# A one-core transformer block with routed experts: ranks from two tiles' counts, normed rows kept on the chip, final half rows loaded last, new order numbers

## The chip, the cores and the metric

The kernel runs on one core of a Trainium2 chip. The metric is device time in microseconds, from the first instruction to the last with what the launch adds; the median of three runs is compared. The core has five engines with queues of their own: PE (TensorE, matrix products), DVE (VectorE), ACT (ScalarE), POOL (GpSimd) and SP (SyncE, which here issues nearly all loads and stores). A queue runs strictly in its order: what stands behind a waiting instruction waits too. 16 DMA engines carry the transfers.

## What is computed

One layer on 1024 latent tokens of 1024 numbers, with 256 context tokens. A normed and modulated input goes through one projection, three groups of token mixers (windowed attention, gated mixing in chunks, differential attention) and an output projection with a gated residual. Behind that stand routed experts and a final norm; the change lies in this half:

```python
y = jnp.concatenate([ya, yb, yc], axis=-1) @ w_out
x = x + gt1 * y
h2 = rmsnorm(x, g_ffn[l]) * (1.0 + sc2) + sh2
...
pg = jax.nn.softmax((t @ w_rg) + b_rg, axis=-1)       # 4 groups, the best one
ptop, gsel = lax.top_k(pg, 1)
...
lv, li = lax.top_k(le_g, MOE_TOPK)                    # 2 of its 4 experts
for e in range(N_EXPERTS):                            # 16
    he = jax.nn.silu(t @ w_gate[e]) * (t @ w_up[e])   # 1024 -> 512
    y = y + gates[:, e:e + 1] * (he @ w_down[e])      # 512 -> 1024
...
x = x + gt2 * y
return rmsnorm(x, g_final)
```

All is float32; products are made exact enough by splitting an operand into a high and a low part, three products for one.

## The kernel before

The first half (to 586.9 us) is the same in both versions. The second half is recorded as steps by `add(engine, estimated us, (key, class), function, reads, writes)`. `Plan.order` then replays them as a list scheduler: of the steps that are ready it takes the one with the least start time plus `weight * (key + shift[class])`, the shifts being the table `SHIFT2`, and writes the instructions of all engines in that order. `key` is a due time by place in the program. Buffers are rings: `F` (1024 columns, 6), `R` (raw weight slabs, 7), `W` (split slabs, 31), `XP`, `he`, `C`, and in PSUM `A` and `T`.

*Tiles.* `out_tile(t)`, eight times 128 tokens: transposes (`turn`, L1081), the output projection as two halves of eight steps of `three` products (L1075 to L1077, two halves n), gate and residual (L1158, L1160), squares on ACT (L1166), inverse root on POOL (L1171 to L1173), norm and modulation on DVE (L1176, L1179), a store of the residual to `accd` (L1169) and of the normed rows to `h2d` (L1180). Then the router: transposes of the normed rows, logits (L1197), group and expert choice on DVE (L1204 to L1231), running counts per expert in `selsum` (`base`, L1234), places by a product with a triangle (L1238, L1239), slot numbers (L1251 to L1257), and two indirect stores that enter token and gate into `table` (`enter`, L1260). For tiles in `AGAIN = (0, 3, 4)` the router's transposes don't read the normed rows where VectorE wrote them, but a copy loaded back from `h2d`; the buffer is free earlier so.

*Ranks.* Experts are worked on by rank, and each rank has a fixed capacity in token rows, `CAPS`: 320, five times 192, seven times 128, three times 64; a loop behind everything (L1690) takes what does not fit. `first_expert` finds rank 0 from the counts of the first `FIRST = 2` tiles, into `oi0`. `rank_experts` ranks all 16 from the counts of `CUT = 6` tiles, with rank 0 kept, into `oi`. `close` pads rank 0's count to `EARLY = 192` rows, so that two early blocks of rank 0 (128 and 64 rows) can be gathered from the tables of six tiles alone; tile 6's `base` waits for it.

*Experts.* Ranks are taken in the order `ORDER` (0, 9, 13, 8, ...). A rank has 24 slabs of 256 KB (8 gate, 8 up, 8 down), all 384 in one chain on SP (`slab`, L1042). Each is split into high and low, on ACT (L1062) and on DVE or POOL (L1039). `expert_block` handles 128 or 64 rows: SP loads its indices from `table` (L1439, after the tables of all tiles but for the early blocks), POOL gathers the rows from `h2d` (L1442), PE transposes them (L1457), ACT and DVE split them (L1469, L1473), then gate, up (L1075 and so on; L1483, L1486 for 64 rows), SiLU (L1498), the gate factor (L1501), down, and POOL adds the result into `accd` (L1445).

*Tail.* `final_tile(t)` loads `accd` after all sums but those of the last rank, norms it and stores it: tiles 0 to 3 through ring `F`, tile 4 through `C`, tiles 5 to 7 as half rows through `R`. The last rank's block does its rows by itself and scatters them over the output when all stores of the tiles have landed.

## Time and profile before

| | us |
|---|---|
| median of 3 runs | 1183.41 (1179.22 to 1183.45) |
| the profiled execution | 1187.16 |
| its span, first to last instruction | 1185.4 |
| second half, from 586.9 to the end | 598.5 |

The profile is one execution. Busy times say how long an engine executed; an idle time stands in brackets in a timeline's row with what ended it. Positions are microseconds from the span's start, lines are those of the kernel before. The TensorE clock has two levels, 1.2 and 2.4 GHz; PEclk is the granted share of the higher. In the second half a row of SP (`SPq`) is the issue of a transfer, not the transfer.

### The profile page before, as it was taken

To read this page: it belongs to the slowest core of one execution; us is meant where nothing else is said; L and a number is where in the kernel's file an instruction comes from. 1 tells how busy PE (TensorE), PEld (TensorE's weight loads), DVE (VectorE), ACT (ScalarE), POOL (GpSimd) and SP (SyncE) were. 2 spreads that over 40 slices of the span, in tenths; PEclk is the share of its full clock that TensorE was granted. 3 is DMA by queue.
4 is the path that set the end of the run, shared out by engine and by line. 5 is a ranking of instruction groups with operands and counts; after the bars stand their busy time and mean duration, and the time that the engine had idled before them with its cause. 6 is when DMAs were issued, how large, how long until landed. Compare 5 with 4: busy or idle time off the path is not lost. (4 is left out here: it accounts for less than half of the span.)

```text
span 1185.4 us, 18587 instructions
## 1 busy us (share of the span) xinstructions
PE 1055.2 (89%) x5621; PEld 833.7 (70%) x5621; DVE 909.9 (77%) x1735; ACT 718.4 (61%) x1443; POOL 414.3 (35%) x452
## 2 busy tenths in 40 slices
PE   6999999977999999999799985899989989899680
PEld 1688677766888888888677874686767767677550
DVE  6665779748788887887757778889886878988865
ACT  6774122118988888988622332377676667777753
POOL 0200000103778788776522534312222313222220
PEclk9899999999999999999989897899989999999895
DMA  9624674010000000000244663589988988899995
GB/s 326 217 80 148 197 236 152 9 41 9 19 1 19 1 1 19 10 4 7 62 143 159 207 198 133 167 270 294 272 297 265 294 282 263 268 288 292 271 317 219
DMA packets 99980, 191.30 MB, mean 161 GB/s; under 512 B 17720, under 2 KB 19560, under 8 KB 99750
## 3 DMA queue, kind: packets, MB, share of 16 engines
q1 hardware_dynamic: 93574, 172.59, 43.8%
q0 software_dynamic: 6272, 17.51, 6.8%
q8 instruction: 45, 0.74, 0.3%
q14 instruction: 57, 0.47, 0.1%
q10 hardware_dynamic: 32, 0.01, 0.0%
HBM read 168.95 MB, written 24.07 MB: 163 GB/s over the span
## 5 line engine op out<-in xcount | busy, mean ns | idle before, releaser
L698 DVE TENSOR_REDUCE st<-SC 128x1 f32<-128x1280 f32 x64 | 95.2, 1487 | 20.8 <-PE SC L693 16.3
L430 PE MATMUL acc<-wh,hH 128*128 128x512 f32 x256 | 101.2, 396 | 1.7 <-ACT bu L530 0.9
L431 PE MATMUL acc<-wl,hH 128*128 128x512 f32 x256 | 100.8, 396 | 0.0
L432 PE MATMUL acc<-wh,hL 128*128 128x512 f32 x256 | 100.3, 392 | 0.0
L1075 PE MATMUL A<-W,XP 128*128 128x512 f32 x236 | 98.6, 418 | 0.6 <-ACT W L1062 0.6
L1076 PE MATMUL A<-W,XP 128*128 128x512 f32 x236 | 95.6, 405 | 1.8 <-DVE W L1039 1.8
L701 ACT ACTIVATE P<-SC,st 128x1280 f32<-128x1280 f32 x64 | 85.2, 1330 | 16.6 <-DVE st L698 15.4
L1077 PE MATMUL A<-W,XP 128*128 128x512 f32 x236 | 95.0, 403 | 0.0
L1062 ACT ACTIVATE W<-R 128x512 fp32r<-128x512 f32 x111 | 69.0, 626 | 27.4 <-DMA R<-in_w_down_dram 7.0
L1039 DVE TENSOR_TENSOR W<-R,W 128x512 fp32r<-128x512 f32 x102 | 69.8, 694 | 18.3 <-ACT W L1062 16.2
L633 ACT ACTIVATE PT<-T 128x512 f32<-128x512 f32 (+1 forms) x126 | 65.2, 546 | 11.3 <-PE T L629 9.5
L745 PE MATMUL T<-vc,PT 128*128 128x64 f32 x512 | 62.2, 275 | 0.3 <-DVE qa L930 0.2
L1445 POOL DMA_INDIRECT accd<-F,IX x18 | 30.8, 1709 | 87.8 <-DVE F L1504 26.5
L745 PEld LDWEIGHTS T<-vc,PT 128*128 128x128 f32 x512 | 59.7, 192 | 0.6 <-ACT PT L633 0.4
L693 PE MATMUL SC<-KC,QC 128*128 128x512 f32 (+1 forms) x192 | 52.4, 381 | 6.6 <-ACT P L701 6.3
L430 PEld LDWEIGHTS acc<-wh,hH 128*128 128x128 f32 x256 | 48.1, 188 | 13.8 <-issue 2.3
L432 PEld LDWEIGHTS acc<-wh,hL 128*128 128x128 f32 x256 | 48.1, 188 | 11.3 <-issue 1.1
L1075 PEld LDWEIGHTS A<-W,XP 128*128 128x128 f32 x236 | 46.3, 196 | 12.9 <-ACT W L1062 1.3
L431 PEld LDWEIGHTS acc<-wl,hH 128*128 128x128 f32 x256 | 48.1, 188 | 10.3 <-issue 0.9
L857 DVE TENSOR_REDUCE ast<-SA 128x1 f32<-128x640 f32 (+1 forms) x64 | 50.2, 784 | 6.0 <-PE SA L850 5.4
L455 DVE SCALAR_TENSOR_TENSOR macc<-mw,cs,macc 128x512 f32<-128x512 f32 x56 | 41.8, 747 | 16.6 <-DMA mw<-in_w_ada_dram 16.2
L1076 PEld LDWEIGHTS A<-W,XP 128*128 128x128 f32 x236 | 46.2, 196 | 11.7 <-DVE W L1039 2.8
(782 smaller groups left out, 3155.5 us busy)
## 6 DMA issues: line engine op xcount, KB each, us to landing
R<-in_w_gate_dram SPq DMA_DIRECT2D x74, 256.0 KB
R<-in_w_down_dram SPq DMA_DIRECT2D x73, 256.0 KB
R<-in_w_up_dram SPq DMA_DIRECT2D x72, 256.0 KB
mw<-in_w_ada_dram SPq DMA_DIRECT2D x64, 256.0 KB
wr<-in_w_in_dram SPq DMA_DIRECT2D x32, 256.0 KB
kc<-in_w_up_dram SPq DMA_DIRECT2D x20, 256.0 KB
kc<-in_w_down_dram SPq DMA_DIRECT2D x19, 256.0 KB
late_vcB<-in_w_gate_dram SPq DMA_DIRECT2D x18, 256.0 KB
```

Of the source, the lines that this page charges most:

```text
L430: nc.tensor.matmul(acc[:, n0:n1], lhsT=a, rhs=W[k][0][:, n0:n1], start=(k == 0), stop=False)
L431: nc.tensor.matmul(acc[:, n0:n1], lhsT=a, rhs=W[k][1][:, n0:n1], start=False, stop=False)
L432: nc.tensor.matmul(acc[:, n0:n1], lhsT=b, rhs=W[k][0][:, n0:n1], start=False, stop=(k == KD - 1))
L633: nc.scalar.activation(dst, src, AF.Copy)
L698: nc.vector.tensor_reduce(small[0][:, j:j + 1], buf(("SC", u, j))[:, 0:1280], axis=AX.X, op=OP.max, negate=True)
L701: nc.scalar.activation(buf(("P%d" % j, u)), buf(("SC", u, j))[:, 0:1280], AF.Exp, bias=small[0][:, j:j + 1], accum_out=small[0][:, 2 + j:3 ...
L745: nc.tensor.matmul(buf(O)[:, 0:64], lhsT=buf(("PT", u, g))[:, (c - c0) * 128:(c - c0 + 1) * 128], rhs=vc[c // 8][:, c % 8, h * 64:(h + 1) ...
L1039: (nc.gpsimd if engine == "POOL" else nc.vector).tensor_sub(dst, a, b)
L1062: h = add("ACT", 0.525, (key, "sh"), lambda: nc.scalar.activation(buf(value)[:, 0:512], raw(), AF.Copy), r=r, w=[value], after=[chain["spl ...
L1075: nc.tensor.matmul(acc, lhsT=ah, rhs=w[:, 0:512], start=first, stop=False)
L1076: nc.tensor.matmul(acc, lhsT=ah, rhs=w[:, 512:1024], start=False, stop=False)
L1077: nc.tensor.matmul(acc, lhsT=al, rhs=w[:, 0:512], start=False, stop=last)
```

## The change

- `AGAIN` is empty: the router's transposes of all tiles read the rows where VectorE wrote them; three loads go.
- `rank_experts` ranks all 16 experts from the counts of the first two tiles (`NB0`); `first_expert`, `oi0` and `lead` go. `close` takes rank 0's count of six tiles from `NB_`.
- The half rows of the final norm (ring `R`) are recorded as coming after the last slab (`after=[chain["load"]]`).
- Classes get finer: the steps of tile 5 (`c`), tile 7 (`z`), of the early blocks (`a`) and the last rank (`z`) have shifts of their own, as have constants and final tiles. All numbers of `SHIFT2` are new, the weight is 8.4e-05 instead of 0.005541, and some estimated times are set anew.

```diff
-SHIFT2 = dict(weight=0.005541, c=-100.3, fa=-315.5, fh=20.8, fl=78.4, fn=-1857.9, fo=545.6, fr=-845.7, fs=276.2,
...
+SHIFT2 = dict(weight=8.4e-05, c0=7509.6, c1=-814.8, c2=10962, c3=3158.7, c4=-4675.7, ex=3038.8, fa=-107164,
...
-AGAIN, LAGR = (0, 3, 4), 8.8
+AGAIN, LAGR = (), 8.8
...
+            own = {CUT - 1: "c", NT - 1: "z"}.get(t, "")
...
-            add("DVE", 1.2, (k, "oh"), lambda: nc.vector.scalar_tensor_tensor(
+            add("DVE", 1.2, (k, "oh" + own), lambda: nc.vector.scalar_tensor_tensor(
...
-        def first_expert():
...
-            nc.vector.tensor_copy(cnt, buf(NB_)[:, :16])
+            nc.vector.tensor_copy(cnt, buf(NB0)[:, :16])
...
-            nc.vector.scalar_tensor_tensor(key, lead, 65536.0, key, op0=OP.mult, op1=OP.add)
...
-            nc.vector.tensor_scalar(gap, cnt, -1.0, float(EARLY), op0=OP.mult, op1=OP.add)
+            nc.vector.tensor_scalar(gap, buf(NB_)[:, :16], -1.0, float(EARLY), op0=OP.mult, op1=OP.add)
...
-        add("DVE", 1.2, (kc_, "k0"), first_expert, r=[NB0], w=["oi0"])
+        add("DVE", 3.1, (kc_, "k0"), rank_experts, r=[NB0], w=["oi"])
...
-        add("DVE", 5.4, (kc_, "k"), rank_experts, r=[NB_, "oi0"], w=["oi"])
-        add("DVE", 0.4, (kc_, "k"), close, r=["oi"], w=["adj"])
+        add("DVE", 0.6, (kc_, "k"), close, r=[NB_, "oi"], w=["adj"])
...
-                load(n * 1.36e-3, (k, "fl"), lambda Y=Y: buf(Y), lambda c=c: accd[rows, c], [Y], r=["sum"])
+                load(n * 1.36e-3, (k, "gl"), lambda Y=Y: buf(Y), lambda c=c: accd[rows, c], [Y], r=["sum"],
+                     after=[chain["load"]] if ring == "R" else [])
```

VectorE, before, about where tile 6 waits for its places: the end of the ranking (L1316 to L1321), gathered rows of the first early block (`XP`, L1473), closing (L1325 to L1327), tile 6's base (L1234, L1235).

```order
L1316 TENSOR_REDUCE rank<-q_5675 128x16
L1317 TENSOR_TENSOR q_5675<-rank,ie 128x256
L1319 TENSOR_TENSOR q_5676<-q_5675,ie 128x256
L1320 TENSOR_REDUCE order<-q_5676 128x16
L1321 CAST oi<-order 128x16
L1473 TENSOR_TENSOR XP_5631<-T_5658,XP_5631 128x512
L1325 TENSOR_SCALAR gap<-cnt 128x16
L1326 SCALAR_TENSOR_TENSOR gap<-gap,q_5675 128x16
L1327 TENSOR_TENSOR selsum<-selsum,gap 1x16
L1234 CAST sel<-selsum 128x16
```

The same place now (new line numbers): the count of six tiles (L1304), the slots of tile 4 (L1264 to L1270, the numbers behind the names tell the tiles apart), closing, the next tile's slots.

```order
L1304 CAST selb<-selsum 128x16
L1264 TENSOR_TENSOR pos<-A_5652,estep 128x16
L1266 TENSOR_TENSOR s_6699<-s_6699,pos 128x32
L1268 TENSOR_REDUCE sl<-s_6699 128x2
L1270 CAST sli<-sl 128x2
L1325 TENSOR_SCALAR gap<-A_5655 128x16
L1326 SCALAR_TENSOR_TENSOR gap<-gap,q_5675 128x16
L1327 TENSOR_TENSOR selsum<-selsum,gap 1x16
L1264 TENSOR_TENSOR pos<-A_5651,estep 128x16
```

Ranking and gathered rows no longer stand ahead of the closing; the ranking stands behind tile 1's base, some 150 rows earlier. Two subtractions of gathered rows (L1472 in the new numbers) now stand between tile 7's base and its slots.

SP, before, where the long run of index loads (`IX`, the first two for the early blocks stand further ahead) begins: slabs of the second expert, whose number is read from `oi`, then the index loads.

```order
L1418 TENSOR_LOAD oi
L1042 ISA
L1042 DMA R_5629<-in_w_gate_dram 128x512
...
L1042 DMA R_5627<-in_w_gate_dram 128x512
...
L1042 DMA kc<-in_w_up_dram 128x512
L1439 ISA
L1439 DMA IX_5597<-table 128x2
```

The same place now: "down" slabs of rank 0, the index loads, and one more "down" slab after the third of them.

```order
L1054 DMA kc<-in_w_down_dram 128x512
L1054 ISA
L1054 DMA R_5626<-in_w_down_dram 128x512
...
L1054 DMA R_5629<-in_w_down_dram 128x512
L1417 TENSOR_LOAD oi
L1438 ISA
L1438 DMA IX_5597<-table 128x2
```

Ahead of this run stood 33 slabs before, 24 of rank 0 and nine of the next expert; now 22 of rank 0. The run had nine index loads, five slabs and eight index loads; now 13 index loads with one slab among them. Of rank 0's slabs, 10 stand ahead of the index loads of the early blocks now, and 24 did before.

SP, before, at the end: the last slab but one (`kc`), the eleven loads of the final norm, the last slab.

```order
L1042 DMA kc<-in_w_down_dram 128x512
L1042 DMA kc<-accd 128x1024
L1042 DMA F_5622<-accd 128x1024
...
L1042 DMA R_5626<-accd 128x512
L1042 DMA R_5629<-accd 128x512
L1042 ISA
L1042 DMA kc<-in_w_down_dram 128x512
L1618 DMA out_dram<-kc 128x1024
```

The same place now: all slabs, then the eleven loads.

```order
L1054 DMA R_5629<-in_w_down_dram 128x512
L1054 ISA
L1054 DMA kv<-in_w_down_dram 128x512
L1054 DMA kc<-accd 128x1024
L1054 DMA F_5619<-accd 128x1024
...
L1054 DMA R_5629<-accd 128x512
L1619 DMA out_dram<-kc 128x1024
```

The last slab moved ahead of the loads of the final norm.

## Rows read from the trace of the kernel before

**Rows 1.** The page's first part: busy time, share of the span, instructions.

```profile
PE 1055.2 (89%) x5621; PEld 833.7 (70%) x5621; DVE 909.9 (77%) x1735; ACT 718.4 (61%) x1443; POOL 414.3 (35%) x452
```

**Rows 2.** Windows: stretch, length, busy by engine (instructions), PEclk, DMA share, GB/s.

```profile
586.90:718.00 131.10, 119.53 (x571) 97.69 (x571) 96.07 (x258) 45.64 (x106) 47.32 (x63) 0.91 0.55 178
718.00:741.80 23.80, 10.05 (x51) 9.49 (x51) 18.74 (x61) 4.29 (x13) 8.20 (x11) 0.61 0.42 146
741.80:777.00 35.20, 32.71 (x154) 25.27 (x155) 29.98 (x93) 15.78 (x27) 11.59 (x14) 0.88 0.57 166
777.00:1143.40 366.40, 339.08 (x1540) 257.02 (x1539) 303.32 (x461) 253.31 (x447) 97.45 (x67) 0.98 0.92 282
1143.40:1185.40 42.00, 10.01 (x30) 5.80 (x29) 22.12 (x37) 18.89 (x42) 3.08 (x3) 0.62 0.68 259
586.90:1185.40 598.50, 511.39 (x2343) 395.27 (x2343) 470.22 (x910) 337.92 (x634) 167.63 (x157) 0.92 0.78 245
```

**Rows 3.** Timeline of PE, tiles and hand-over: start, us, what, [idle before <- releaser].

```profile
592.21 0.69 PE L1081 MATMUL T<-ident,he 128*128 128x128 f32 x2 [0.97 <-DMA he<-bud]
597.83 0.69 PE L1081 MATMUL T<-ident,he 128*128 128x128 f32 x2 [1.94 <-DMA he<-bud]
...
692.64 1.12 PE L1081 MATMUL T<-ident,F 128*128 128x128 f32 x4 [3.92 <-DMA F<-h2d]
...
717.52 0.39 PE L1077 MATMUL A<-W,XP 128*128 128x512 f32 x1
...
728.70 1.97 PE L1081 MATMUL T<-ident,F 128*128 128x128 f32 x8 [2.24 <-DVE F L1179]
...
741.82 1.97 PE L1457 MATMUL T<-ident,F 128*128 128x128 f32 x8 [7.64 <-DMA F<-h2d,IX]
```

**Rows 4.** Timeline of SP's queue, then its slab issues in the middle by source line.

```profile
712.41 0.33 SPq L1042 DMA_DIRECT2D R<-in_w_down_dram  x1
...
756.66 6.62 SPq L1439 DMA_DIRECT2D IX<-table  x9
...
769.26 6.47 SPq L1439 DMA_DIRECT2D IX<-table  x8
...
777.18 0.33 SPq L1042 DMA_DIRECT2D kv<-in_w_down_dram  x1
...
L1042 SPq FUSED_REGOPS  x342: 42/46/110, 777.6 to 1142.9; - x171
```

**Rows 5.** Timeline of VectorE and GpSimd, routing of the last tiles.

```profile
735.41 0.17 DVE L1309 COPY cnt<-A 128x16 f32<-128x16 f32 x1
...
743.60 0.69 DVE L1473 TENSOR_TENSOR XP<-T,XP 128x512 fp32r<-128x512 f32 x1 [5.11 <-ACT XP L1469]
...
744.21 0.17 DVE L1325 TENSOR_SCALAR gap<-cnt 128x16 f32<-128x16 f32 x1
...
754.52 0.96 POOL L1260 DMA_INDIRECT table<-ent,sli  x1 [0.21 <-issue]
```

**Rows 6.** Timeline of the tail, SP's queue, PE and GpSimd.

```profile
1143.45 0.33 SPq L1042 DMA_DIRECT2D kc<-in_w_down_dram  x1
...
1144.94 0.33 SPq L1042 DMA_DIRECT2D kc<-accd  x1
...
1155.43 0.34 SPq L1042 DMA_DIRECT2D kc<-in_w_down_dram  x1
...
1165.32 0.80 PE L1075 MATMUL A<-late_bu,WX 128*128 128x512 f32 x1 [12.39 <-ACT late_bu L1062]
...
1171.17 1.02 POOL L1445 DMA_INDIRECT accd<-F,IX  x1 [24.95 <-DMA out_dram<-R]
1174.21 0.98 POOL L1445 DMA_INDIRECT out_dram<-kc,IX  x1 [2.01 <-DVEq L1690]
```

**Rows 7.** Windows of 25 us inside the middle, columns as in rows 2.

```profile
975.00:1000.00 25.00, 24.67 (x118) 18.54 (x118) 20.87 (x31) 17.04 (x31) 8.56 (x6) 1.00 0.87 260
...
1075.00:1100.00 25.00, 21.33 (x96) 14.90 (x94) 21.78 (x35) 18.04 (x34) 2.80 (x2) 1.00 0.93 297
```

More of the change, by code (lines that the diff above doesn't have):

```diff
@@ L1198, in logits @@
                                      stop=(k == KD - 1))
-            chain["lg", t] = add("PE", 1.72, (k, "ol"), logits, r=[HT], w=[LG])
+            chain["lg", t] = add("PE", 1.72, (k, "ol" + own), logits, r=[HT], w=[LG])
             lg = lgs[:, t, :]
@@ L1286, in block_kernel @@
         oi = rc.tile([128, 16], I32)
-        oi0 = rc.tile([128, 1], I32)
-        lead = one.tile([128, 16], F32)
         nc.vector.tensor_scalar(ie, estep, 1.0 / STRIDE, None, op0=OP.mult)
@@ L1516, in expert_block @@
             half = m == 64
+            tag = "a" if early else "z" if late else ""
             XG, XP, HP, HE, YE = ("F", "xg", j), ("XP", "x", j), ("W", "hp", j), ("he", "h", j), ("F", "ye", j)
             k0 = key(0)
-            add("SP", 0.45, (k0 - 14, "ix"), lambda: B.index(expert_of(r) * STRIDE + slot, buf(("IX", j))),
-                r=["oi" if r else "oi0"] + [("tab", t, i) for t in range(CUT if early else NT) for i in range(2)], w=[("IX", j)], dma=(0.05, 1.0, 0.5))
-            add("POOL", 1.1, (k0 - 9, "xg"), lambda: B.gather(buf(XG), h2d, CUT * 128 if early else SEQ),
-                r=[("IX", j)] + [("h2d", t) for t in range(CUT if early else NT)], w=[XG], dma=(m * 0.0164, 2.6, 2.1),
+            add("SP", 0.45, (k0 - 14, "ix" + tag), lambda: B.index(expert_of(r) * STRIDE + slot, buf(("IX", j))),
+                r=["oi"] + [("tab", t, i) for t in range(CUT if early else NT) for i in range(2)], w=[("IX", j)], dma=(0.05, 1.0, 0.5))
+            add("POOL", 1.1, (k0 - 9, "xg" + tag), lambda: B.gather(buf(XG), h2d, CUT * 128 if early else SEQ),
+                r=[("IX", j)] + [("h2d", t) for t in range(CUT if early else NT)], w=[XG], dma=(m * 0.0156, 2.6, 2.1),
                 after=[chain["x", j - 2]] if j > 1 else [])
@@ L1561, in expert_block @@
                 if half:
[L1562 to L1564 removed]
+                    add("ACT", 0.5, (k, "fh" + tag), lambda acc=acc, TMP=TMP: B.fold_high(buf(TMP), buf(acc)), r=[acc], w=[TMP])
+                    add("DVE", 0.6, (k, "fl" + tag), lambda acc=acc, TMP=TMP: B.fold(buf(TMP), buf(TMP), buf(acc)), r=[acc], w=[TMP])
+                add("DVE", 0.6, (k, "yg" + tag), lambda acc=acc, TMP=TMP, c=c: B.times_gate(
                     buf(YE), buf(TMP) if half else buf(acc), c, const("gt2")), r=[TMP if half else acc, ("C", "gt2")], w=[YE])
             if not late:
[L1567 to L1568 removed]
+                add("POOL", 1.75, (kd, "ys" + tag), lambda: B.scatter(accd[:, :], buf(YE), compute_op=OP.add),
+                    r=[YE, ("IX", j)] + [("acc", t) for t in range(NT)], w=["sum"], dma=(m * 0.0234, 2.6, 2.7))
                 return
@@ L1579, in expert_block @@
             chain["late"].append(j)
-            add("POOL", 1.1, (kd - 12, "xa"), lambda: B.gather(buf(XA), accd), r=["sum", ("IX", j)] + before, w=[XA], dma=(m * 0.0164, 2.6, 2.1))
+            add("POOL", 1.1, (kd - 12, "xa"), lambda: B.gather(buf(XA), accd), r=["sum", ("IX", j)] + before, w=[XA], dma=(m * 0.0156, 2.6, 2.1))
             add("DVE", 1.15, (kd, "fa"), lambda: nc.vector.tensor_add(buf(XA)[:m], buf(XA)[:m], buf(YE)[:m]), w=[XA, YE], port=True)
@@ L1631, in block_kernel @@
             for i, (name, k) in enumerate(SLABS):
-                slab(("W", r, name, k), start + i * max(step, 0.9) - LEAD, lambda r=r, name=name, k=k: weight(expert_of(r), name, k), ["oi" if r else "oi0"],
-                     "POOL" if i in (POOLED if r else POOLED0) else "DVE")
+                slab(("W", r, name, k), start + i * max(step, 0.9) - LEAD, lambda r=r, name=name, k=k: weight(expert_of(r), name, k), ["oi"],
+                     "POOL" if i in (POOLED if r else POOLED0) else "DVE",
+                     "z" if r == ORDER[-1] else "a" if r == 0 else "")
             slot = 0
```

133 lines of the change are left out of this document (66 added, 67 removed).

## The prediction

> **What bounds the kernel now.** I read the page first, then the windows of the last stage, then the waits of TensorE in it, and the queue of SyncE beside them. The page shows TensorE at 89% and VectorE at 77% of the span [rows 1]. The diff changes nothing ahead of the block layer's second half (output projection, routing, experts), which begins at 586.9 us, so only the 598.5 us behind that can move. The windows cut them into five stretches [rows 2]: the eight tiles of the output projection (131.1 us, clock 0.91), the hand-over to the experts (23.8 us with TensorE busy for 10.1, clock 0.61), the first expert (35.2 us, DMA share 0.57), the middle (366.4 us, TensorE busy 339.1 of it, DMA share 0.92, 282 GB/s) and the tail (42.0 us, TensorE busy 10.0). The middle is nearly full on two sides at once; the losses to be had lie around it.
>
> In the tiles TensorE waits for the column of normed rows read back from DRAM, 3.92 us at tile 4, and for two early loads, 0.97 and 1.94 us [rows 3]. The last product of tile 7 ends at 717.9 us (717.52 + 0.39); its transposes for the router start 10.8 us later, at 728.70, and the first gathered expert rows reach TensorE at 741.82 after 7.64 us of idling [rows 3]. Meanwhile SP's queue has loaded the 24 slabs of rank 0 by 712.41; it then knows no other expert until the ranking is done. The long run of index loads starts at 756.66, that is 38.8 us after the last product, nine loads in 6.62 us (0.74 us each), then eight more at 769.26; from 777 on slabs flow [rows 4]. 41 of the 384 slabs are issued by then, 59.2 us after the last product, and 342 follow in 366 us, 1.07 us each [rows 4].
>
> **The change, part by part.** The sum is made against the profiled execution, 1187.16 us (span 1185.4); the median of the three timed runs, 1183.41, is 3.75 us lower, and the forecast subtracts the same gain from it.
>
> *Normed rows not read back* (tiles 0, 3 and 4). Three loads of 512 KB go, with SP's three issues. The wait of 3.92 us goes with them [rows 3]; tiles 0 and 3 read no wait near that size. The transposes now read the buffer that VectorE wrote; what is late next there is VectorE's own addition, which feeds them in the other five tiles already. In the new order the three constants come behind the output weights instead of ahead of them, and the first loads of the tiles come first, so of 0.97 + 1.94 us I count half, 1.5. With fewer gaps some of the clock comes back: 0.09 of 131.1 us is 11.8 us lost now; I take a fifth, 2.5. Together **8 us** for the tiles; from 0 (new waits of another kind) to 14.
>
> *Ranking by the counts of two tiles.* The full ranking replaces the short search for the first expert after tile 1, and the counts of six tiles only set how far the first expert's early slots are padded. In the old order VectorE starts the ranking at 735.41, then stands 5.11 us at 743.60 for the gathered rows of the first block, and only at 744.21 closes the early slots, on which tiles 6 and 7 wait for their places; the last table entry is issued at 754.52 [rows 5]. In the new order closing stands ahead of tile 5's slots and of any gathered row, and the ranking is long done. The 8.8 us from 735.41 to 744.21 leave that chain; tile 6's and 7's routing no longer queue behind tile 5's, for which I take 4 us more, an estimate from the 36.6 us between the last product and the last entry. So entries end about 24 us after the last product and the long run of index loads begins at about 26, not 38.8. Against that: the new order has only 22 slabs ahead of it (the old one 33), and in it 13 index loads with one slab between them: 13 x 0.74 = 9.6 us. Slabs flow again from 35.6 us with 23 issued; the 18 that make up the old 41 take 18 x 1.07 = 19.3, so the same count is reached 54.9 us after the last product instead of 59.2: **4 us**. The price of the wait has two ends: if entries end as late as now, 38.8 + 9.6 + 19.3 = 67.7, 8.5 us worse; if the tables land at 16, 14 us better.
>
> The ranks themselves change. The reference's router on its inputs gives, by the new ranks, 300, 192, 180, 131, 163, 175, 118, 108, 117, 86, 125, 113, 86, 61, 51 and 42 rows, all within the capacities 320, 5 x 192, 7 x 128, 3 x 64 (rank 1 exactly full, as it is now). No spill block is due, and the padding is zero in both (231 early rows, 192 wanted).
>
> *Half rows of the final norm behind the last slab.* Now the last "down" slab is issued at 1155.43, eleven final-norm loads after the one before it at 1143.45; TensorE stands 12.39 us for it, and the last scatter leaves at 1174.21 [rows 6]. But the final rows are a second chain: they start at 1144.94, as soon as all sums have landed, and their last store has landed when GpSimd is let go at 1171.17 [rows 6]; the last scatter waits for all of them too. So of the 12.39 us only what the last expert is later than the rows, 1174.21 - 1171.17 = 3.0 us, and the 1.0 us of the slab in the rows' stream (0.262 MB at the tail's 259 GB/s [rows 2]) can come off; the slab then costs 1.07 in the middle. What is late next is the rows' own traffic. **3 us**, from 0 to 5.
>
> *The new numbers for the order.* The weight falls 66-fold while the shifts grow as much, so place in the program counts little and class nearly everything; the first and last expert's steps get numbers of their own. In the middle this reorders all, and nothing in the old trace prices it. Bounds from rows: the middle's 103 MB at the pace of a slow 25-us window (260 GB/s) would take 397 us, at that of a fast one (297) 348, so +31 to -18 [rows 7]; I take 0, since both TensorE's and the DMA's shares are over 0.9 and the work is the same.
>
> Sum: 8 + 4 + 3 = 15. Profiled 1172; median 1183.4 - 15 = **1168.4 us**.
>
> One page bears on the middle. The row shows a DMA share of 0.92 at 282 GB/s [rows 2]. The Trainium skill, "Perfetto Trace Analysis", section "Identifying the Most-Contended Engine", says that with 16 engines occupancy misleads for DMA and bytes per time should be used; "DMA: Bandwidth & Descriptors", section "Bandwidth", gives 425 GB/s for 16 MB from one core. By these the middle isn't held by DMA, and a better order could quicken it; that is the first rival.
>
> **Rivals.** (1) *The middle quickens*: its pace is set by how the order hands ring slots back, not by the engines. For it speaks that a 25-us window reaches 297 GB/s [rows 7]; against it TensorE's 339.1 busy us of 366.4, which leave 27 us at most. At 348 us: 1168.4 - 18 = 1150. Chance 0.15. (2) *The middle eats the gain*: the greedy order leaves TensorE waiting for split slabs more often. At 4% (about halfway to the slow window), 366.4 x 0.04 = 14.7, so 1183: no change. Chance 0.17. (3) *Slower*: the old trap in a new place. In the new order VectorE has two subtractions of gathered rows between tile 7's base and its slots, as it stood 5.11 us for one at 743.60 [rows 5]; if the early gather is late, tile 7's entries, the 13 index loads behind them on SP and 361 slabs behind those wait for it. The gather reached TensorE 7.6 us late in the old trace [rows 3]. With entries landing 45 us after the last product the 41 slabs are reached at 45 + 9.6 + 19.3 = 73.9, 14.7 later than now, and if the tiles give nothing either, 1183.4 + 14.7 - 3 = 1195. It decides above some 38 us (38 + 28.9 - 59.2 = 7.7 worse, less 3 at the tail: 1188). Against it: the gather waits for tile 5 alone, whose routing is finished before tile 7's products end. Chance 0.09. (4) *The change doesn't do what it says*: two tiles rank wrongly on the chip, and a spill block runs alone at the end, 24 slabs of at least 1.07 us, over 26 us: 1195 or more. Rank 1 is full to the row, but equally so before. Chance 0.02.
>
> **How the numbers follow.** Forecast 0.57, its own range 1156 to 1177 (the three terms rarely all at one end); rivals as above. About 0.5%, 6 us, is what a measurement can tell from none. Faster, below 1177.5: nearly all of the forecast, with rival 1, makes 0.71; within 0.5%: 0.18; slower: 0.11. The range reaches a little past rival 2, to 1186, and past rival 1, to 1148; outside it lie the two slower rivals and the ends of rivals 1 and 2, some 2 in 10.
>
> **What would show it.** Right: no read of the normed rows; the last tile product at about 710 us instead of 717.9; index loads beginning 24 to 28 us behind it; no wait over 5 us of TensorE for a slab in the tail; about 40 us from the last slab's issue to the end; the middle's slabs at 1.05 to 1.09 us each. Wrong: a stand of VectorE for gathered rows ahead of tile 7's slots; a middle with a DMA share under 0.88 or over 0.96; new waits of TensorE in the tiles; a loop of the spill block at the end.

## The result, and the profile after

The changed kernel takes **1199.1 us** (median of four runs, 1193.4 to 1204.9) against 1181.6 for the kernel before beside it (1179.2 to 1183.5). The ratio is 1.0143, with an interval of 1.0098 to 1.0189. The prediction said 1168.4 us, faster; the kernel is slower by 1.4%, and outside the range. The profiled execution of the changed kernel took 1193.4 us (span 1191.4), the shortest of its four runs, and that of the kernel before took longer than its median. So only 6.0 of the 17.5 us between the medians stand between the two traces.

The windows of the changed kernel over the same stretches of time, columns as in [rows 2]:

```profile
586.90:718.00 131.10, 121.90 (x616) 100.84 (x615) 96.97 (x302) 40.56 (x99) 40.74 (x64) 0.93 0.46 157
718.00:741.80 23.80, 16.56 (x68) 12.26 (x69) 21.48 (x62) 9.21 (x18) 15.59 (x18) 0.73 0.58 165
741.80:777.00 35.20, 29.97 (x137) 23.91 (x136) 28.10 (x50) 19.81 (x35) 5.32 (x5) 0.95 0.79 251
777.00:1143.40 366.40, 332.49 (x1481) 250.00 (x1480) 294.64 (x450) 244.32 (x433) 93.98 (x67) 0.95 0.90 273
1143.40:1185.40 42.00, 11.99 (x39) 8.08 (x37) 22.88 (x37) 21.08 (x45) 4.60 (x4) 0.63 0.73 275
```

By 777 us TensorE has done 821 instructions where it had done 776; over the next 366.4 us it does 59 fewer, its clock is 0.95 for 0.98, and 273 GB/s flow for 282. The early part gained and the middle lost. TensorE's timeline at the end of the tiles, and SyncE's queue behind it, beside [rows 3, 4]:

```profile
703.29 0.39 PE L1089 MATMUL A<-W,XP 128*128 128x512 f32 x1
...
710.70 1.97 PE L1093 MATMUL T<-ident,F 128*128 128x128 f32 x8 [0.39 <-DVE F L1192]
...
723.99 1.97 PE L1456 MATMUL T<-ident,kc 128*128 128x128 f32 x8 [7.79 <-issue]
```

```profile
735.78 1.75 SPq L1438 DMA_DIRECT2D IX<-table  x3
737.80 0.33 SPq L1054 DMA_DIRECT2D kc<-in_w_down_dram  x1
738.64 7.75 SPq L1438 DMA_DIRECT2D IX<-table  x10
...
747.20 0.36 SPq L1054 DMA_DIRECT2D late_vcB<-in_w_down_dram  x1
```

The last tile product is 14.2 us earlier than in [rows 3], the index loads begin 20.9 us earlier than in [rows 4], and slabs flow from 747 instead of 777. The 41st slab leaves at 761.6 us, where it was 777.2: a lead of 15.6 us. The last slab but one:

```profile
1146.48 0.33 SPq L1054 DMA_DIRECT2D R<-in_w_down_dram  x1
```

In [rows 6] it was 1143.45. The lead is gone by then: 384.9 us for 342 slabs, 1.13 us each instead of 1.07 (366.3 us), so the middle costs 18.6. From there to the end of the span it is 44.9 us, and was 41.9. The ledger of the two profiled spans is thus 15.6 us gained, 18.6 lost in the middle and 2.9 lost in the tail: +6.0 us, which is their difference.

### The profile page after: what moved, and what is told of

Same layout as the page of the kernel before. It is cut to its first block, busy times and chain, and to the rows that moved or that the text cites. A ratio compares the mean times of both kernels' runs of the same rounds, so it can differ in the third digit from the quotient of the medians.

```text
span 1191.4 us, 18506 instructions
## 1 busy us (share of the span) xinstructions
PE 1059.8 (89%) x5621; PEld 837.1 (70%) x5621; DVE 904.6 (76%) x1728; ACT 718.7 (60%) x1443; POOL 408.9 (34%) x452
## 5 line engine op out<-in xcount | busy, mean ns | idle before, releaser
L1087 PE MATMUL A<-W,XP 128*128 128x512 f32 x226 | 91.9, 407 | 2.9 <-DVE F L1503 2.2
L1088 PE MATMUL A<-W,XP 128*128 128x512 f32 x226 | 89.9, 398 | 2.5 <-POOL W L1051 2.1
L1089 PE MATMUL A<-W,XP 128*128 128x512 f32 x226 | 89.2, 395 | 0.0
L1074 ACT ACTIVATE W<-R 128x512 fp32r<-128x512 f32 x111 | 68.8, 627 | 33.0 <-DMA R<-in_w_up_dram 14.2
L1051 DVE TENSOR_TENSOR W<-R,W 128x512 fp32r<-128x512 f32 x102 | 72.2, 720 | 9.7 <-ACT W L1074 7.2
L1444 POOL DMA_INDIRECT accd<-F,IX x16 | 27.6, 1726 | 84.8 <-DVE F L1581 29.4
L1087 PEld LDWEIGHTS A<-W,XP 128*128 128x128 f32 x226 | 43.3, 192 | 14.7 <-ACT W L1074 4.0
L467 DVE SCALAR_TENSOR_TENSOR macc<-mw,cs,macc 128x512 f32<-128x512 f32 x56 | 41.8, 747 | 14.7 <-DMA mw<-in_w_ada_dram 14.4
L1088 PEld LDWEIGHTS A<-W,XP 128*128 128x128 f32 x226 | 43.3, 192 | 12.7 <-POOL W L1051 3.2
```

What stands on the lines that cost most here:

```text
L1051: (nc.gpsimd if engine == "POOL" else nc.vector).tensor_sub(dst, a, b)
L1074: h = add("ACT", 0.525, (key, "sh" + name), lambda: nc.scalar.activation(buf(value)[:, 0:512], raw(), AF.Copy), r=r, w=[value], after=[cha ...
L1087: nc.tensor.matmul(acc, lhsT=ah, rhs=w[:, 0:512], start=first, stop=False)
L1088: nc.tensor.matmul(acc, lhsT=ah, rhs=w[:, 512:1024], start=False, stop=False)
L1089: nc.tensor.matmul(acc, lhsT=al, rhs=w[:, 0:512], start=False, stop=last)
```

## The experiments

Two kinds of reading return below: the time of a kernel, and how its slabs flow. The table has the times at which SyncE issues the 41st expert slab and the last but one, read from the timeline of its queue (to 1 us), the time per slab between them, and the median time. A span ends 41 to 66 us behind the last slab but one.

```
                          41st  last but one  us/slab   median
before                    777   1143          1.07      1181.6
after                     762   1146          1.13      1199.1
e1  old numbers           780   1151          1.09      1204.9
e2  two edits undone      779   1179          1.17      1224.3
e3  old numbers, middle   781   1187          1.19      1251.4
e4  rows free             764   1149          1.13      1196.3
e5  rows alone            775   1143          1.08      1185.1
e6  estimates alone       787   1174          1.13      1227.2
e9  new to 41, then old   767   1139          1.09      1183.4
e10 new to 160, then old  767   1152          1.12      1195.2
e11 old to 41, then new   773   1170          1.16      1211.3
e17 new to 24, then old   776   1141          1.07      1185.6
e18 new to 100, then old  767   1147          1.11      1189.5
```

The kernel before, run beside each of them, stood at 1181.2 to 1184.4 us.

### The numbers, the edits, or the early start

The first theory (N) was that the new numbers order the middle badly. Against it stood S, that the edits themselves (the ranking above all) do it, and H, that an early start is given back in any order.

e1 is the kernel before with the three edits, planned with the old numbers and old estimated times:

```diff
-AGAIN, LAGR = (0, 3, 4), 8.8
+AGAIN, LAGR = (), 8.8
...
-        add("DVE", 1.2, (kc_, "k0"), first_expert, r=[NB0], w=["oi0"])
+        add("DVE", 3.1, (kc_, "k0"), rank_experts, r=[NB0], w=["oi"])
...
+                     after=[chain["load"]] if ring == "R" else [])
```

> The three edits of the code (no read back, ranking by two tiles, half rows behind the last slab) with the order made by the numbers of the kernel before. Theory N (the new numbers cost the middle): the slabs from 777 us to the last one pass at 1.06 to 1.08 us each as before, and the time is 1172 to 1182 us. Rival S (the edits themselves, the ranking above all, cost the middle): slabs at 1.10 us or more, 1190 to 1200 us. Rival H (an earlier start of the slabs is worth nothing, since the middle gives it back whatever the order): 1180 to 1185 us, with slabs the slower the earlier they start.

1204.9 us, ratio 1.0182 (1.0102 to 1.0262). No expectation holds: the old numbers, so good for the kernel before, make the edited kernel slower than the new ones do, and even its early lead is missing. Its middle runs at 1.09 us a slab; most of its loss lies behind that, 54.8 us from the last slab but one to the end for 41.9.

e2 keeps the new numbers and undoes two edits (the ranking and the rows' place):

```diff
-        add("DVE", 3.1, (kc_, "k0"), rank_experts, r=[NB0], w=["oi"])
+        add("DVE", 1.2, (kc_, "k0"), first_expert, r=[NB0], w=["oi0"])
...
-                     after=[chain["load"]] if ring == "R" else [])
```

> The changed kernel with the ranking by two tiles and the half rows behind the last slab undone; the new numbers and the missing read back stay. Theory N: the middle stays slow, 1.09 us or more a slab, and the time is 1195 to 1212 us, as changed or later, since the index loads again wait for the full ranking behind tile 5. Rival S: a middle at 1.07 us and 1180 to 1188 us. Rival H: 1185 to 1195 us.

1224.3 us, 1.0345 (1.025 to 1.0441), above the ranges of all three theories: the new numbers are even worse for nearly the old kernel than the old ones are for the new.

e3 mixes them: old numbers for the middle's steps, new ones for the rest.

```diff
-        rank = [weight * (s[2][0] + self.shift.get(s[2][1], 0.0)) for s in self.steps]
+        rank = [weight * (s[2][0] + self.shift.get(s[2][1], 0.0)) if self.shift is not SHIFT2 or s[2][1] not in OLDS
+                else OLD2["weight"] * (s[2][0] + old(s[2][1])) for s in self.steps]
```

> The changed kernel with the old numbers (weight and shifts) for the slabs and blocks of the experts between the first and the last; tiles, first expert and last expert keep the new ones. Theory N: slabs flow from about 747 us as in the changed kernel and at 1.06 to 1.08 us each, so the last leaves some 12 to 20 us earlier than its 1147 us, and the time is 1172 to 1183 us. Rival S: 1190 to 1200 us, as changed. Rival H: slabs start at 747 us but take 1.10 us each; 1185 to 1200 us.

1251.4 us, 1.0574 (1.0489 to 1.0658), the slowest order of all, and in no theory's range. So theory N can't be tested by the numbers: a mixture isn't the old order in the middle, it is a third order. The early lead falls with it.

e4 undoes one edit, and here the order stays the same, tail included: in the two traces each engine has the same sequence of instructions, and SyncE issues the rows' loads behind the last slab all the same.

```diff
-                load(n * 1.36e-3, (k, "gl"), lambda Y=Y: buf(Y), lambda c=c: accd[rows, c], [Y], r=["sum"],
-                     after=[chain["load"]] if ring == "R" else [])
+                load(n * 1.36e-3, (k, "gl"), lambda Y=Y: buf(Y), lambda c=c: accd[rows, c], [Y], r=["sum"])
```

> The changed kernel with the final rows' loads again free to go ahead of the last slab; nothing else differs. Theory N: the middle is as slow as in the changed kernel, the time within 1190 to 1204 us; the stand of TensorE for the last slabs decides about 4 us at most. A rival T (the tail holds the loss: the rows' loads behind the last slab keep the end 44 us behind it) expects 1180 to 1186 us.

1196.3 us, 1.0117 (1.0036 to 1.0199), and the middle as slow as in the changed kernel. As no instruction moved, this repeats the changed kernel and doesn't test theory T. The two traces speak against T: from the last slab but one to the end it is 44.9 us in both, 3 more than before, where the middle loses 19.

e5 is the same edit alone in the kernel before, where the order is also the same up to the tail.

> The kernel before with one edit alone: the half rows of the final norm load behind the last slab. Up to the tail the order is the same. The prediction's term: 3 us gained, 1178.5 us against 1181.5. Rival: the final rows are the chain that decides, and they now start later by what the slab is late (it waits for its ring slot to be split, until about 1150 us), so 2 to 8 us are lost, 1184 to 1190 us.

1185.1 us, ratio 1.0014 (0.9987 to 1.0042): nothing, and neither expectation. SyncE's queue, TensorE and GpSimd in its tail, beside [rows 6]:

```profile
1147.33 0.52 SPq L1042 DMA_DIRECT2D kv<-in_w_down_dram  x1
...
1154.61 0.32 SPq L1042 DMA_DIRECT2D kc<-accd  x1
...
1170.47 0.33 SPq L1619 DMA_DIRECT2D out_dram<-kc  x1
```

```profile
1158.91 0.79 PE L1075 MATMUL A<-late_bu,WX 128*128 128x512 f32 x1 [6.17 <-ACT late_bu L1062]
```

```profile
1165.24 1.01 POOL L1445 DMA_INDIRECT accd<-F,IX  x1 [19.68 <-DMA out_dram<-kv]
1173.83 0.98 POOL L1445 DMA_INDIRECT out_dram<-kc,IX  x1 [7.58 <-SPq L1691]
```

The last slab leaves 8.1 us earlier, TensorE stands 6.17 us instead of 12.39, and the last expert's sum leaves 5.9 us earlier. But the last half rows are now loaded at 1154.61 and stored at 1170.47, SyncE comes to the end of its queue later than before, and the last scatter waits 7.58 us for it: it leaves 0.4 us earlier than before. The slab and the rows change places, and the tail stays as long.

e6 changes nothing but twelve lines of durations by which the plan is made; the numbers, the work and the data moved are those of before.

```diff
-            us = 0.456 if half else 0.684
+            us = 0.466 if half else 0.7
```

> The kernel before with nothing changed but the durations by which its order is planned (a turn of four 0.40 for 0.36 us, a product 0.70 for 0.684, gathers and scatters a tenth shorter, and so on, as in the changed kernel); the numbers, the work and the data moved are the same. Theory F (the order of before fits the chip because its numbers were fitted to exactly this plan, and any new plan is an ordinary one): 1190 to 1210 us, the loss between 777 us and the last slab and in the tail. Rival (an order changed a little costs little): 1178 to 1186 us.

**1227.2 us, ratio 1.0388 (1.0327 to 1.0449)**: 44 us for a new plan of the same work. That is theory F's direction and beyond its range; in the trace 10 of the 36 us more are already lost at the 41st slab, where F named the middle and the tail only. An order that comes from these numbers isn't a little different when something about it changes a little: it is another one, and of the four new plans up to here that were made with numbers meant for another one (e1, e2, e3, e6) none has a median under 1204 us.

### The order cut and joined

So the order has to be held fixed. In e9, e10, e11, e17 and e18 it is given as a list of steps: one kernel's order up to the nth expert slab, word for word, and behind it the other's. The planner only hands out the buffers.

```diff
+        place = {x: p for p, x in enumerate(FORCED)} if n == len(FORCED) else None
...
-                c = (t + rank[i], i, t, s)
+                c = (t + rank[i] if place is None else place[i], i, t, s)
```

> The changed kernel (its code and work) in an order given as a list: word for word that of the changed kernel up to the 41st expert slab's load, and from there on the steps in the order of the kernel before. Theory N (the loss lies in the order of the steps behind the first expert): 41 slabs at about 762 us, the next 342 at 1.07 to 1.08 us each, the last but one at 1128 to 1133 us, the time 1166 to 1175 us. Rival S (the changed ranking or the missing read back cost the middle): 1.10 us or more a slab, 1190 to 1200 us. Rival H (an early start is given back in any order): 1180 to 1185 us.

> The opposite: the code and work of the kernel before, its order up to the 41st slab, and from there the order of the changed kernel. Theory N: 41 slabs at about 778 us as before, then 1.10 to 1.13 us each, the last but one at 1155 to 1165 us, the time 1200 to 1212 us. Rival S: the middle as before, 1180 to 1186 us. Rival H: 1190 to 1197 us.

e9 takes 1183.4 us, ratio 0.9991 (0.9958 to 1.0024); e11, which has the code and the work of before, takes 1211.3, ratio 1.0231 (1.017 to 1.0291). The windows of the middle, of e9 and then of e11:

```profile
777.00:1143.40 366.40, 335.13 (x1529) 254.26 (x1528) 302.44 (x460) 253.38 (x447) 98.49 (x68) 0.98 0.91 280
```

```profile
777.00:1143.40 366.40, 328.02 (x1443) 246.25 (x1442) 285.52 (x434) 234.40 (x416) 90.12 (x64) 0.94 0.86 262
```

With the old order behind the 41st slab the changed kernel's middle reads nearly as in [rows 2]; with the new order the old kernel's middle loses 97 instructions of TensorE. **The loss goes with the order, and with no edit**: S falls, and N holds for where the loss lies. The new order behind the 41st slab costs 16 us in the changed kernel (1199.1 - 1183.4) and 27 in the old one.

But H is half right too. e9 starts the middle with a lead of 10 us and isn't faster than before. Slabs 41 to 60 take 24 us in it (18 before), and from there on both run at 1.08 us a slab, with 4 us between them at the last but one. Most of the loss lies at the seam itself, in SyncE's queue:

```profile
767.33 0.70 SPq L1162 DMA_DIRECT2D R<-in_w_down_dram  x1
768.76 2.90 SPq L1546 DMA_DIRECT2D IX<-table  x4
772.15 0.34 SPq L1162 DMA_DIRECT2D kc<-in_w_down_dram  x1
```

The new order has 16 of the 23 index loads ahead of its 41st slab, the old one 19. e9 issues four of them behind the seam, and its lead falls from 9.9 to 5.6 us between the 41st slab and the 42nd. So a lead counted in slabs is in part other work put off. TensorE's count fits this: by 777 us e9 has done 797 of its instructions, before 776, and 21 at the 0.23 us that lie between two starts in an undisturbed row of matmuls make 5 us. That a lead is kept only as far as TensorE has moved with it is argued, not shown.

e17 and e18 move the seam of e9, e10 puts it where the changed kernel's trace showed its lead melting:

> As e9, with the seam behind the 24th expert slab: the changed kernel's order for the tiles, the routing, the index loads and the first expert's slabs, that of before from there on. If the lead of 11 us at the 41st slab was lost at the seam of e9: 1170 to 1179 us. If it is lost in any order, because what the lead brings has to wait for TensorE and VectorE in the old order: 1180 to 1186 us, as e9.

> As e9, with the seam behind the 100th slab. If seams themselves cost (e10's 30 slabs behind its seam took 39 us): 30 to 40 us for the 30 slabs behind the seam, then the old pace, and 1183 to 1195 us. If they don't: 1172 to 1180 us.

> The same with the seam behind the 160th slab: the changed kernel's order up to there (about 891 us, 11 us ahead of before), then that of before. Theory N: 1172 to 1180 us; the 8 us lost between the 160th and the 190th slab don't occur. Rival S: 1190 to 1200 us. Rival H: 1180 to 1185 us.

(e10's label has its two orders the wrong way round; its expectation says it right.) They take 1185.6 us (1.0042; 1.0018 to 1.0065), 1189.5 (1.0055; 1.0037 to 1.0074) and 1195.2 (1.0095; 1.0068 to 1.0122). From the 41st slab on, the later the old order takes over, the slower. Part of that is the stretch left to the new order: e10's lead is 10 us at the 41st slab and 2 at the 160th. Part is the seam: the 30 slabs behind it take 36 us in e10 and 38 in e18, where they took 31 and 33 in the kernel before. So seams at these two places cost some 5 us. No version with all of the work beats the kernel before.

### What an order can lose there

Open was how an order can cost that much in a stretch in which TensorE and the DMA were both over 0.9 busy before and at 0.9 now. The following leave out work and keep the order, instruction by instruction. e7 and e12 leave out the products with the low half of the weights, in the changed kernel and in the one before:

```diff
-                    three(acc, h[:, k, :], l[:, k, :], w[k], first, last)
+                    nc.tensor.matmul(acc, lhsT=h[:, k, :], rhs=w[k][:, 0:512], start=first, stop=False)
+                    nc.tensor.matmul(acc, lhsT=l[:, k, :], rhs=w[k][:, 0:512], start=False, stop=last)
...
-                for f in ((rest, main) if last else (main, rest)):
-                    f()
+                main()
```

> The changed kernel with the expert products' second part left out (the low half of the weights: two matmuls instead of three for 128 rows, one instead of two for 64); every other instruction stands in the same order. Theory P (TensorE's work sets the middle): slabs at 0.95 us or less instead of 1.11, and 1125 to 1145 us. Theory R (the ring of slab buffers sets it: landing, the two splits, the next issue): slabs stay at 1.08 us or more, 1180 to 1195 us. Both in turn, each standing behind the other in the fixed order: 1.00 to 1.05 us a slab and 1150 to 1175 us.

> The kernel before with the expert products' second part left out, as was done with the changed kernel; the order is otherwise the same. If the ring of slab buffers with its two splits sets the pace in the order of before too: 1.06 to 1.08 us a slab and 1175 to 1190 us. If TensorE's work sets it there: 1.00 us or less and 1140 to 1160 us.

1199.2 us and 1185.3 us (ratios to the kernel before 1.0134, 1.0094 to 1.0173, and 1.0018, 0.9984 to 1.0052): **a third of TensorE's products in the middle is worth nothing, in either order.** The middle of e7 and of e12:

```profile
777.00:1143.40 366.40, 256.36 (x986) 186.65 (x985) 294.44 (x448) 242.22 (x432) 100.03 (x67) 0.82 0.88 269
```

```profile
777.00:1143.40 366.40, 260.11 (x1020) 191.91 (x1019) 302.30 (x458) 250.93 (x442) 96.30 (x67) 0.82 0.91 277
```

TensorE stands for over 100 us, its clock falls to 0.82, and the slabs flow at 1.14 and 1.08 us, with all products at 1.13 and 1.07.

e8 loads half of each slab:

```diff
-            chain["load"] = load(0.685, (key, "ld" + name), lambda: buf(R), src, [R], r,
+            chain["load"] = load(0.685, (key, "ld" + name), lambda: buf(R)[0:64], lambda: src()[0:64], [R], r,
```

> The changed kernel with half of each expert slab loaded (64 of its 128 rows; the buffers are set to zero once, and the rest of the work is done on what stands there), in the same order. Theory P: the slabs' pace stays above 1.05 us, 1180 to 1195 us. Theory R: 0.95 us or less and 1120 to 1145 us. Both in turn: 1.00 to 1.05 us and 1150 to 1175 us.

The same function loads part of the output projection's weights, so the routing changed as well, blocks of the spill loop ran at the end, and the 1370.3 us of the whole say nothing. Up to the 360th slab the kernel can be compared: from the 41st it takes 347 us, against 360 in the changed kernel, 4%. The windows from 777 to 1110 us, of the changed kernel and of e8:

```profile
777.00:1110.00 333.00, 304.30 (x1370) 228.50 (x1369) 269.01 (x411) 222.50 (x397) 86.59 (x62) 0.96 0.89 272
```

```profile
777.00:1110.00 333.00, 310.92 (x1417) 234.95 (x1416) 278.26 (x427) 227.40 (x414) 100.68 (x65) 0.97 0.69 162
```

Next the two splits of each slab, first the low part alone (e13), then the high part alone (e14), then both (e15), and at last all of it together with the fewer products and the half slabs (e16; the output projection's weights in full):

```diff
-                engine, buf(value)[:, 512:1024], raw(), f32(buf(value)[:, 0:512])), r=r, w=[value], port=True)
+                engine, buf(value)[:, 512:512 + n], raw()[:, 0:n], f32(buf(value)[:, 0:n])), r=r, w=[value], port=True)
```

> The changed kernel with the low half of each expert slab split over 64 of its 512 columns (VectorE and GpSimd), except where a buffer is filled for the first time; order, loads and products as before. Theory V (VectorE's queue, 80% busy, sets the pace): 0.95 us a slab or less and 1145 us or less. Theory L (each engine stands in turn for another's latency in the fixed order; no engine's work is the bound): 1.05 us or more and 1175 to 1195 us.

> The same for the high half, which ScalarE takes: 64 of 512 columns. Theory A (ScalarE's queue sets the pace): 0.95 us a slab or less. Theory L and theory V: 1.05 us or more, 1175 to 1195 us.

> Both halves short. What both engines' work is worth together: under theory V or A at most 0.95 us a slab; if TensorE's work or the loads come next as bounds, about 0.98 to 1.03 us (TensorE's busy time of 339 us over 342 slabs is 0.99); theory L: 1.03 us or more, 1165 to 1190 us.

> Both splits short, two products instead of three (one instead of two for 64 rows), and half of each expert slab loaded: every engine's share of the slab work is cut, and the latencies and the order stay. Theory L: still 0.85 us or more a slab, 1090 us or more; if work sets the pace, 0.6 us or less and 1010 us or less.

```
                       us/slab  median   ratio to before
after                  1.13     1199.1   1.0143 (1.0098 to 1.0189)
e13 low parts short    1.09     1179.6   0.9964 (0.9938 to 0.9991)
e14 high parts short   1.10     1201.2   1.0173 (1.0109 to 1.0236)
e15 both short         1.07     1172.5   0.9893 (0.9861 to 0.9925)
e16 all short          0.94     1136.1   0.9605 (0.9556 to 0.9653)
```

The middles of e13, e14 and e15, and of e16 up to its last slab but one:

```profile
777.00:1143.40 366.40, 331.62 (x1495) 250.69 (x1493) 166.02 (x460) 249.01 (x444) 62.61 (x69) 0.96 0.91 284
```

```profile
777.00:1143.40 366.40, 335.98 (x1507) 252.66 (x1506) 299.13 (x455) 140.13 (x440) 110.02 (x69) 0.96 0.90 277
```

```profile
777.00:1143.40 366.40, 339.21 (x1516) 256.53 (x1515) 164.65 (x468) 146.02 (x458) 63.77 (x69) 0.95 0.93 291
```

```profile
777.00:1089.00 312.00, 234.83 (x999) 175.44 (x998) 158.22 (x450) 135.76 (x433) 62.60 (x68) 0.90 0.78 185
```

VectorE's busy time falls by 129 us (294.64 to 166.02), and 19.5 us come off the whole; ScalarE's falls by 104, and nothing comes off; both together give 27. With every engine's share of the slab work cut, TensorE is busy for 75% of the stretch, VectorE for 51 and ScalarE for 44, and a slab still takes 0.94 us, of which TensorE, the busiest, works 0.71. So theories P, V and A fall as bounds, VectorE's work being the one that counts for something: **no single engine's work sets the middle's pace.** Two theories are left. L says that it is set by steps that wait for one another in a fixed order. R says that the ring of seven slab buffers sets it; e12 came out as the ring would have it, and e8 hardly tested R, since with half of the bytes a slab's first split begins 5.06 us after its issue instead of 5.69.

The traces show that the ring is the loop in which these waits run. In slabs 42 to 360, when SyncE issues one, six earlier ones have not been split to the end yet in 309 of 319 cases before and in 312 now, and the issue follows the end of the last split of the slab seven places before by 0.03 us in the median. A slab leaves when a buffer comes free, and the pace is a seventh of a buffer's round. Means over these slabs, in us, worked out from the rows of each slab's issue and of its two splits:

```
                                  before   after   e16
issue to start of high split       5.60     5.69   4.61
high split                         0.63     0.63   0.27
its end to the end of low split    1.18     1.47   0.71
to the buffer's next issue         0.10     0.13   1.10
round, and a seventh of it    7.51 1.07  7.91 1.13  6.69 0.96
```

Of the 0.40 us that a round is longer now, 0.29 lie between the two splits: where the low split is VectorE's (293 of the 319), it starts 0.71 us behind the end of the high one, and 0.41 before. In e16 (0.94 us a slab over all 342) most of a round lies ahead of the first split. How much of that is the landing and how much ScalarE's queue can't be read from the rows, and no run has more buffers.

How such waits look can be seen in the changed kernel at 910 us, here on TensorE, then ScalarE, VectorE, GpSimd and SyncE's queue:

```profile
909.82 0.40 PE L1089 MATMUL A<-late_shared,W 128*128 128x512 f32 x1
914.65 0.71 PE L1456 MATMUL T<-ident,F 64*128 64x64 f32 x8 [4.43 <-DVE XP L1472]
915.29 0.73 PE L1087 MATMUL A<-W,W 128*128 128x512 f32 x1
```

```profile
911.24 0.63 ACT L1074 ACTIVATE late_qc<-kc 128x512 fp32r<-128x512 f32 x1 [3.83 <-DMA kc<-in_w_gate_dram]
912.75 0.63 ACT L1074 ACTIVATE WX<-R 128x512 fp32r<-128x512 f32 x1 [0.89 <-DMA R<-in_w_gate_dram]
913.29 0.58 ACT L1468 ACTIVATE XP<-T 128x512 fp32r<-128x512 f32 x1
```

```profile
911.90 0.69 DVE L1051 TENSOR_TENSOR late_qc<-kc,late_qc 128x512 fp32r<-128x512 f32 x1 [3.53 <-ACT late_qc L1074]
913.90 0.69 DVE L1472 TENSOR_TENSOR XP<-T,XP 128x512 fp32r<-128x512 f32 x1 [1.31 <-ACT XP L1468]
```

```profile
902.24 1.33 POOL L1441 DMA_INDIRECT F<-h2d,IX  x1 [0.16 <-issue]
903.88 0.99 POOL L1441 DMA_INDIRECT kc<-h2d,IX  x1 [0.31 <-issue]
```

```profile
903.51 0.09 SPq L1054 DMA_DIRECT2D kc<-in_w_gate_dram  x1
...
912.62 0.33 SPq L1054 DMA_DIRECT2D kc<-in_w_gate_dram  x1
```

TensorE transposes gathered rows and needs a PSUM buffer of an earlier turn, which VectorE frees at 914.6. VectorE waited for ScalarE's copy of it (913.29), and ScalarE's copy stood in its queue behind two slab splits, the first of which waited 3.83 us for a slab. That slab was issued at 903.51, just as GpSimd issued two gathers; its low split ends at 912.59, and 0.03 us later the next slab goes into its buffer, after a round of 9.1 us. TensorE stands 4.43 us, and its next product takes 0.73 us instead of 0.40. In the list the copy comes behind the two splits, and whether that costs depends on when a slab lands on the chip. That the two gathers held the slab up is argued, not shown. It goes the other way as well, in the waits of ScalarE from 777 to 1147 us, of the changed kernel and of before (total, times, longest):

```profile
ACT W L1468 <- PE T L1456: 19.1, 11, 3.0
ACT late_shared L1468 <- PE T L1456: 4.3, 3, 2.0
ACT XP L1468 <- PE T L1456: 3.7, 5, 1.6
```

```profile
ACT W L1469 <- PE T L1457: 5.2, 5, 1.5
ACT late_bu L1469 <- PE T L1457: 1.9, 1, 1.9
ACT late_qc L1469 <- PE T L1457: 1.7, 1, 1.7
```

Here ScalarE stands for a transpose of TensorE while slab splits wait behind it. With the smaller rows it is 31.5 us in all, and was 11.6. No run takes single stands of this kind away, so how the 18.6 us of the middle divide among them stays open.

## Why the prediction was wrong, step by step

**The tiles** (8 us, from 0 to 14). Right, and at the upper end: no read of normed rows is left, no wait for an early load either, and the last tile product ends at 703.7, 14.2 us earlier than in [rows 3]. The prediction's list said about 710. 2.8 us of it lie ahead of the tiles, whose first transpose runs at 584.94, and at 587.78 before.

**The hand-over** (4 us). The mechanism was right, its size too large. The last table entry is issued 28.8 us behind the last product (24 predicted, 36.6 before), the index loads begin 32.1 us behind it (26; 38.8), and the 41st slab leaves 58 us behind it (54.9; 59.2): 1 us instead of 4. The thirteen index loads with one slab between them came as read from the order, 9.5 us of issuing for the 9.6 predicted. Both terms together promised a lead of 12 us at the 41st slab, and 15.6 were there. Rival 3 didn't happen: VectorE subtracts the gathered rows at 726.04 without a stand.

**What the lead is worth** is the first step that failed. The sum counted each us by which slabs flow earlier as one us off the end, with the old pace behind it. e9 is the prediction's own case, new early part and old pace, and it takes 1183.4 us, not 1171 or so: with a lead of 10 us at the 41st slab 4 are left at the last but one, and in the medians 1. Part of the error is that the sum counted slabs alone: the index loads that the new order puts off behind the 41st slab have to be issued too, and 4.3 us of e9's lead go there. The rest is not taken apart, as e9 has a seam as well. e17 has the same tiles and hand-over, next to no lead at the 41st slab (1 us), and 1185.6 us.

**The middle** (0, bounds +31 and -18) is the step that cost most. It measured +18.6 us in the profiled run, and 16 and 27 in the seam runs: inside the bounds, and far from the value taken. The reason given was that TensorE's and the DMA's shares were over 0.9 and the work the same. e7, e12 and e8 show that neither share was a limit: a third of the products was worth nothing, half of the bytes 4%. What sets the pace is the round of the slab buffers, 7.91 us instead of 7.51, and the order sets the waits in it. There "the same work" says nothing on the time, and e6 shows what another order of the same work can cost, 44 us. Rival 2 came nearest, with a price of 14.7 us and a chance of 0.17 that was too small. It blamed waits of TensorE, which e7 shows to cost nothing by themselves; it also let the lead count in full, and so came to 1183.

One page bore on it. The windows show TensorE busy for 339 of 366 us, its weight loads for 257 and VectorE for 303 [rows 2]. The Trainium skill, "Perfetto Trace Analysis", section "Identifying the Most-Contended Engine", warns that busy time of matmuls is no good measure of how near TensorE is to its limit, and that occupancy misleads for DMA; e12 and e8 agree, the first with 0 us for a third of the products, the second with a DMA share of 0.69 that carries 162 GB/s where 0.89 carried 272. The same section of the Trainium skill says to optimize the most contended engine first, which it picks by occupancy for VectorE and by the weight loads' busy share, beside the matmuls' work against its peak, for TensorE. By these rows VectorE comes ahead of TensorE, and e13, with 129 us of VectorE's work gone, gains 19.5 us, where e7 and e14 gain nothing. The prediction drew rival 1 from this page, that a better order could quicken the middle; no order found here does.

**The tail** (3 us off, and 40 us from the last slab's issue to the end). It is 44.0 us, and from the last slab but one 44.9 for 41.9. SyncE's queue, TensorE and GpSimd of the changed kernel, beside [rows 6]:

```profile
1147.39 0.33 SPq L1054 DMA_DIRECT2D kv<-in_w_down_dram  x1
1147.89 0.33 SPq L1054 DMA_DIRECT2D kc<-accd  x1
...
1174.00 0.99 SPq L1619 DMA_DIRECT2D out_dram<-R  x2
```

```profile
1155.13 1.11 PE L1456 MATMUL T<-ident,he 128*128 128x128 f32 x4 [6.95 <-DVE he L1500]
```

```profile
1177.37 1.02 POOL L1444 DMA_INDIRECT accd<-F,IX  x1 [29.43 <-DVE F L1581]
1180.46 0.98 POOL L1444 DMA_INDIRECT out_dram<-F,IX  x1 [2.06 <-DVEq L1692]
```

The rows are stored as late as the slab allows, and still they are done first: GpSimd waits for VectorE's sum of the last expert, whose SiLU stood on ScalarE behind all the splits, the last of which began at 1153.06 when the last slab had landed. So "no wait of TensorE over 5 us for a slab" held to the letter, and 6.95 us for the SiLU took its place. The prediction let the slab and the rows gain separately; e5, the edit alone, shows that they trade places, with 0 us in sum. The 2.9 us come with the new numbers, since they put the rows behind the last slab without the edit too: e4 has the same order and the same 44.9 us.

**The signs** given for a wrong forecast missed. The DMA share was to be under 0.88 or over 0.96 and is 0.90; the slabs' own time, 1.13 us where 1.05 to 1.09 was named, told it.

## What to carry to other kernels

Where one list fixes what every queue does, a stretch in which all engines look nearly full can be paced by the round of its buffers and by the waits that the list puts into it: leave out a third of an engine's work, in the same order, before its busy share is taken for a limit. A planner's numbers fit one plan of one kernel, so an edit measured with a new plan measures the plan (here 20 to 70 us) and not the edit: hold the order fixed, join old and new at a seam, and value the edit there. And a lead counted in loads is not yet a lead: look at what the new order has put off to get it.

## What was not expected of the hardware

- In e7 and e12 TensorE's granted clock over the middle is 0.82, where it was 0.95 and 0.98: with a third fewer products the gaps between them grew, and the rest ran slower. The time stayed: 1199.2 us for 1199.1, and 1185.3 for 1184.4 beside it.
- With half of the bytes per slab the DMA engines' busy share falls from 0.89 to 0.69 only, and with all work cut (e16) it is still 0.78 at 185 GB/s.
- Executions of one order drift apart: with the same list up to there, the 160th slab leaves at 891 us in the changed kernel's trace, at 897 in that of e4 and at 901 in that of e10. The changed kernel's four runs spread over 11.5 us. The kernel before stayed within 4.2 in the four runs beside it, and spread over 14.8 in the seven beside e1.
